# A pooling, attention and convolution backbone: the first layer's scale and shift columns as float32 matmuls with two moving columns, and the second layer's sums at other places

## The chip, the core and the metric

The program runs on one core of a Trainium2 chip. The metric is the device time of one execution in microseconds (us); lower is better. The core has five engines with a queue each: PE (matrix products; its loading of stationary operands is shown apart as PEld), DVE (VectorE), ACT (ScalarE), POOL (GpSimd) and SP, which here issues the transfers between the memory of the chip and that of the core. Each engine works through its own queue in order and waits there for what another engine has to deliver.

## What is computed

Four layers work on 1024 latent tokens with 1024 features; 256 context tokens go along through layers 0 and 1. Each layer normalises, applies a scale and a shift that depend on a condition vector, mixes the tokens, and adds the result back through a gate. The change touches only where scale, shift and gate come from, in layers 0 and 1.

```python
def _modulation(cond, w, b):
    m = jax.nn.silu(cond) @ w + b
    return jnp.split(m, 3, axis=-1)          # shift, scale, gate

shift, scale, gate = _modulation(c, ada_w[i], ada_b[i])
hx = _rmsnorm(x, norm_g[i]) * (1.0 + scale[:, None]) + shift[:, None]
cshift, cscale, cgate = _modulation(c_ctx, ada_w[i], ada_b[i])
hc = _rmsnorm(ctx, norm_g[i]) * (1.0 + cscale) + cshift
...
yx = _pool_mixer(hx, pool_w_in[j], pool_w_grp[j], pool_scale[j], pool_w_out[j])
x = x + gate[:, None] * yx
```

Layer 0 is a pooling layer: `h @ w_in` gives u and g (2048 features), u is averaged over windows of 2, 4, 8 and 16 tokens by groups of features, multiplied by `w_grp` and by silu(g), and projected by `w_out`. Layer 1 is the attention.

## The kernel before

Features lie on the 128 partitions in 8 tiles (k = 0 to 7), tokens along the rows. A float32 product is made of three products of a high and a low part (`mm3`, lines 115 to 117): a gemm of one output tile is 8 x 3 matmuls of 512 columns. The tokens are worked on in two halves of 512 (chunks 0 and 1) and the context of 256 ("c").

A column of the modulation, 128 numbers for feature tile j and one condition, is one VectorE instruction: `ada_tile` (lines 157 to 168) reads a [128, 1024] tile of the transposed weight (512 KB), multiplies it by silu of the condition, which lies on all partitions as `sil["x"]` or `sil["c"]`, and sums along the row, with the bias as start. In the trace it is `junk<-... L166`. Layer 0 has 8 scale tiles (8 to 15), 8 shift tiles (0 to 7) and 8 gate tiles (16 to 23), each for the tokens and for the context.

`consts` loads the two conditions as rows and spreads them over the partitions by four matmuls (line 569). `start` then writes out by hand what all engines but PE do, and PE's order is that of the program throughout:

- a loop over k (line 740) multiplies chunk 0 by the first five weight tiles (`FIRST`), one block of 15 matmuls per k. Ahead of block k stand the scale column of tile k + 2 (`gain`: a sum and L174), and the high and low part of the scaled x (`high` L698 on ACT, `low` L702 on DVE). The context's scale sums lie between them (`EARLY`, line 739).
- then five gemms of chunk 1 (line 822), and between them `step(k)`: the shift column of tile k for the tokens on VectorE (`ada`), and for the context on VectorE for k in 4, 6, 7 (`DV`), else as a product on GpSimd (L793) that ACT sums (L798). `rstd_chain` (lines 245 to 272) makes the inverse norms out of column sums (L240) with 12 small VectorE instructions, among which lie low parts of chunk 1; `rstd_spread` (L278) spreads them.
- then the gemms of the context for these five tiles (`shift_c` and `gained_c` make their operand; L80 of 2 columns, L805, L806).

From there `pool_in` goes on with the other eleven weight tiles; there a scheduler orders all engines but PE. Each weight tile that is fetched (`weight`, line 82) issues its transfer, is split into high and low (L79, L80), and then lets `background` do so many steps as `bg_rate` says: one step is one more modulation tile, a transfer of 512 KB and one or two sums. The steps come from `ada_all`: layer 0's gates (8 tiles, 16 sums), layer 1's scale and shift (16 tiles, 32 sums), layer 1's gate (8 tiles, 8 sums). `RATES` (line 495) holds the rate for each weight tile. Weights and modulation tiles share a ring of three buffers, `raw`. After `pool_in` come the output projection of layer 0 (`out_proj`, one step per weight tile) and layer 1.

## Time and profile before

| | |
|---|---|
| median of 3 runs | 1948.54 us (1943.30, 1948.54, 1949.06) |
| the profiled execution | 1943.86 us |
| its span from the first to the last instruction | 1942.1 us |
| PE busy in the span | 1864.4 us (96%) |
| DVE busy in the span | 1095.8 us (56%) |
| mean granted clock of TensorE | 0.985 of full speed |

The trace gives each instruction a start, a duration and an engine, and names what ended an engine's wait. TensorE's clock has two levels, 2.4 GHz (1.00 in the profile) and 1.2 GHz (0.50); the granted clock of a stretch is the mean over it. A float32 matmul that isn't split in high and low parts leaves two records per instruction, which is why four of them are counted as x8.

### The profile page before, as it was taken

To read this page: it belongs to the slowest core of one execution; us is meant where nothing else is said; L and a number is where in the kernel's file an instruction comes from. 1 tells how busy PE (TensorE), PEld (TensorE's weight loads), DVE (VectorE), ACT (ScalarE), POOL (GpSimd) and SP (SyncE) were. 2 spreads that over 40 slices of the span, in tenths; PEclk is the share of its full clock that TensorE was granted. 3 is DMA by queue.
4 is the path that set the end of the run, shared out by engine and by line. 5 is a ranking of instruction groups with operands and counts; after the bars stand their busy time and mean duration, and the time that the engine had idled before them with its cause. 6 is when DMAs were issued, how large, how long until landed. Compare 5 with 4: busy or idle time off the path is not lost.

```text
span 1942.1 us, 27112 instructions
## 1 busy us (share of the span) xinstructions
PE 1864.4 (96%) x9936; PEld 1604.0 (83%) x9936; DVE 1095.8 (56%) x2251; ACT 729.1 (38%) x1401; POOL 571.1 (29%) x552
## 2 busy tenths in 40 slices
PE   7888899999999999999998999999999999999997
PEld 4677778889998889999997877788888887888887
DVE  7989977256431066667666678544323346432627
ACT  3332215245122155666666555222212225322422
POOL 4645312652110033444433443100000024433120
PEclk9989999999999999999999999999999999999999
DMA  6233351554763466676677646443111165011234
GB/s 253 76 108 99 114 190 60 188 161 142 247 231 108 144 186 191 193 210 188 197 200 216 188 154 221 128 129 118 44 55 44 55 184 179 2 49 49 72 122 153
DMA packets 126960, 274.21 MB, mean 141 GB/s; under 512 B 12874, under 2 KB 48458, under 8 KB 126828
## 3 DMA queue, kind: packets, MB, share of 16 engines
q1 hardware_dynamic: 126828, 272.49, 44.9%
q8 instruction: 78, 1.28, 0.3%
q14 instruction: 54, 0.44, 0.1%
HBM read 218.63 MB, written 53.81 MB: 140 GB/s over the span
## 4 chain that ended last, share of the span: by engine, by line
PE 76%; DVE 12%; DMA 6%; issue 3%; POOL 2%; ACT 1%; SPq 0%; DVEq 0%; POOLq 0%; ACTq 0%
PE mm L117 22%; PE mm L115 21%; PE mm L116 21%; DVE junk L166 4%; PE T L1211 3%; PE O L1237 2%; PE O L1236 2%; DMA raw<-in_ada 2%; PE S L1154 1%; DVE S L455 1%; PE S L1155 1%; POOL S L455 1%; DMA a<-in_xT 1%; PE SC L1157 1%; PE SC L1156 1%
## 5 line engine op out<-in xcount | busy, mean ns | idle before, releaser
L115 PE MATMUL mm<-a,whi 128*128 128x512 f32 (+2 forms) x2160 | 819.9, 380 | 22.3 <-DVE U L418 10.0
L116 PE MATMUL mm<-a,whi 128*128 128x512 f32 (+2 forms) x2149 | 804.3, 374 | 10.9 <-DVE a L80 8.5
L117 PE MATMUL mm<-a,wlo 128*128 128x512 f32 (+2 forms) x2160 | 807.1, 374 | 3.5 <-POOL wlo L80 2.4
L115 PEld LDWEIGHTS mm<-a,whi 128*128 128x128 f32 x2160 | 411.5, 191 | 94.7 <-DVE U L418 11.3
L116 PEld LDWEIGHTS mm<-a,whi 128*128 128x128 f32 x2149 | 409.4, 190 | 81.0 <-DVE a L80 10.1
L117 PEld LDWEIGHTS mm<-a,wlo 128*128 128x128 f32 x2160 | 410.8, 190 | 77.9 <-POOL wlo L80 3.7
L80 POOL TENSOR_TENSOR wlo<-raw,whi 128x256 fp32r<-128x256 f32 (+2 forms) x150 | 191.0, 1288 | 382.5 <-ACT whi L79 341.9
L79 ACT ACTIVATE whi<-raw 128x1024 fp32r<-128x1024 f32 (+2 forms) x237 | 170.9, 738 | 352.1 <-PE mm L116 273.6
L166 DVE CUSTOM_DVE_ANT_0 junk<-raw,sil_x,vec 128x1024 bf16<-128x1024 f32 x86 | 117.9, 1371 | 94.4 <-DMA raw<-in_ada 94.1
L80 DVE TENSOR_TENSOR wlo<-raw,whi 128x1024 fp32r<-128x1024 f32 (+1 forms) x87 | 107.6, 1238 | 112.7 <-ACT whi L79 111.2
L1190 POOL TENSOR_SCALAR pr<-pr,rsum 128x640 f32<-128x640 f32 (+1 forms) x128 | 99.8, 779 | 238.8 <-DVE rsum L1189 188.2
L115 PE MATMUL mm<-a,a 128*128 128x512 f32 (+2 forms) x280 | 97.5, 348 | 7.4 <-ACT a L698 6.3
L1181 ACT ACTIVATE pr<-lg,nmx 128x640 f32<-128x640 f32 (+1 forms) x128 | 102.3, 799 | 2.6 <-DVE nmx L1171 1.6
L224 POOL TENSOR_TENSOR a<-a,a 128x512 f32<-128x512 f32 x42 | 59.9, 1425 | 144.2 <-ACT a L223 138.0
L116 PE MATMUL mm<-a,a 128*128 128x512 f32 (+2 forms) x275 | 95.8, 348 | 4.9 <-DVE a L702 4.9
L117 PE MATMUL mm<-a,a 128*128 128x512 f32 (+2 forms) x280 | 96.4, 344 | 0.5 <-DVE a L80 0.5
L1169 DVE TENSOR_SCALAR_CACHE_REDUCE lg<-SC 128x256 f32<-128x256 f32 x128 | 54.2, 423 | 72.9 <-PE SC L1157 72.8
L1220 DVE TENSOR_TENSOR ptlo<-T,pthi 128x512 fp32r<-128x512 f32 x128 | 88.2, 689 | 10.6 <-ACT pthi L1215 8.6
L1236 PE MATMUL O<-pthi,a 128*128 128x256 f32 x352 | 89.0, 286 | 3.2 <-ACT pthi L1215 3.2
L1237 PE MATMUL O<-ptlo,a 128*128 128x256 f32 x352 | 89.6, 289 | 1.1 <-DVE ptlo L1220 0.6
L1215 ACT ACTIVATE pthi<-T 128x512 fp32r<-128x512 f32 x128 | 76.4, 597 | 20.6 <-PE T L1211 19.5
L1211 PE MATMUL T<-ident,pr 128*128 128x128 f32 x512 | 77.6, 274 | 0.0
(182 smaller groups left out, 2495.0 us busy)
## 6 DMA issues: line engine op xcount, KB each, us to landing
raw<-in_ada SPq DMA_DIRECT2D x86, 512.0 KB
raw<-in_pool_out SPq DMA_DIRECT2D x32, 512.0 KB
raw<-in_conv_in SPq DMA_DIRECT2D x32, 512.0 KB
raw<-in_pool_in SPq DMA_DIRECT2D x27, 512.0 KB
x<-a SPq DMA_DIRECT2D x48, 256.0 KB
raw<-in_na_in SPq DMA_DIRECT2D x24, 512.0 KB
a<-dk SPq DMA_DIRECT2D x48, 256.0 KB
dv<-v SPq DMA_DIRECT2D x40, 256.0 KB
```

What stands on the lines that cost most here:

```text
L79: self.nc.scalar.activation(hi, src, AF.Copy)
L80: (lo_engine or self.nc.vector).tensor_tensor(lo, src, hi.bitcast(F32), op=ALU.subtract)
L115: t.matmul(ps, wh, hh, start=(begin and k == ks[0]), stop=False)
L116: t.matmul(ps, wh, hl, start=False, stop=False)
L117: t.matmul(ps, wl, hh, start=False, stop=(end and k == ks[-1]))
L166: nc.vector.tensor_tensor_reduce(out=junk[:], in0=raw[:], in1=self.sil[c][:], scale=1.0, scalar=self.vec[:, b:b + 1], op0=ALU.mult, op1=AL ...
L1181: nc.scalar.activation(pr[:, :L + CTX], lg[:, :L + CTX], AF.Exp, bias=nm[:], scale=-1.0, accum_out=sm[:])
L1190: nc.gpsimd.tensor_scalar(pr[:, :L], pr[:, :L], rs[:], 1.0, op0=ALU.mult, op1=ALU.mult)
L1211: nc.tensor.transpose(T[:, (s - b0) * P:(s - b0 + 1) * P], pr[:, o:o + P], self.ident[:])
L1220: nc.vector.tensor_tensor(lv, tv, hv.bitcast(F32), op=ALU.subtract)
L1236: nc.tensor.matmul(ops[:], v, hi[:, s, :], start=(n == 0), stop=False)
L1237: nc.tensor.matmul(ops[:], v, lo[:, s, :], start=False, stop=(n == len(seq) - 1))
```

## The change

1. The first layer's scale and shift columns are matmuls. `ada_product` multiplies a [128, 1024] tile of the untransposed weight (a new input, `ada0`, with the features of the condition on the partitions) as eight stationary 128 x 128 operands by `cols`, which holds silu of both conditions as two columns per feature tile. All is float32, the eight matmuls add up in one PSUM bank, and both conditions come out at once. One VectorE instruction per tile then adds the bias and, for the scale, multiplies by the norm's weight.
2. `gain(k + 1)` stands ahead of block k, where it was `gain(k + 2)`; the transfers at the start have another order, and one small transfer (`condT`) is new.
3. `RATES` and the rates at the group weights are lower, so that part of layer 1's sums falls into the output projection.

```diff
+    def ada_product(self, raw):
+        ps = self.bank()[:, 0:2]
+        for q in range(KT):
+            self.nc.tensor.matmul(ps, raw[:, q * P:(q + 1) * P], self.cols[:, 2 * q:2 * q + 2], start=q == 0, stop=q == KT - 1)
+        return ps
...
-        RATES = (0,0,0,0,3,0,5,4,3,0,6,5,5,5,8,6) if 'c' in chunks else (3, 0, 6, 6) * 4
+        RATES = (0,0,0,0,2,0,0,2,2,0,2,2,2,2,3,3) if 'c' in chunks else (3, 0, 6, 6) * 4
...
-                self.bg_rate = (3,0,0,1)[k // 2] if 'c' in chunks else 0
+                self.bg_rate = 0
...
+        self.cols = self.pc.tile([P, 2 * KT], F32, name="cols")
+        nc.sync.dma_start(self.cols[:], i["condT"])
...
+        nc.scalar.activation(self.cols[:], self.cols[:], AF.Silu)
...
         def gain(k):
-            self.ada_tile(0, ["x"], KT + k, raws[k])
-            self.gain(0, "x", k, k + 1)
+            ps = self.ada_product(raws.pop(k))
+            nc.vector.tensor_scalar(self.gains[:, :, k], ps, up[:, k:k + 1], self.vec[:, V_NG + k:V_NG + k + 1],
+                                    op0=ALU.add, op1=ALU.mult)
...
-            for q in EARLY.get(k, ()):
-                self.ada_tile(0, ["c"], KT + q, raws.pop(q))
-            if k + 2 < KT:
-                gain(k + 2)
-                high(0, x0, k + 2)
-                low(0, x0, k + 2)
+            if k + 1 < KT:
+                gain(k + 1)
+                high(0, x0, k + 1)
+                low(0, x0, k + 1)
...
-        def ada(k):
-            raw = shifts[k]
-            self.ada_tile(0, ["x", "c"] if k in DV else ["x"], k, raw)
-            if k not in DV:
-                nc.gpsimd.tensor_tensor(raw[:], raw[:], row[:], op=ALU.mult)
...
-        DV = (4,6,7,)
+        def step(k):
+            ps = self.ada_product(shifts.pop(k))
+            nc.vector.tensor_scalar(self.shifts[:, :, k], ps, self.vec[:, V_AB + k:V_AB + k + 1], None, op0=ALU.add)
...
-                for k in list(raws):
-                    self.ada_tile(0, ["c"], KT + k, raws.pop(k))
-                self.gain(0, "c")
```

In the order of the changed program, PE between the spreading of the conditions (L578 there, mm_150 and mm_151 are two of its four banks) and the second block of chunk 0 (a_207 is the scaled x of tile 0, whi and wlo the weight):

```order
L578 MATMUL mm_150<-a_137,ones 128x512
L578 MATMUL mm_151<-a_137,ones 128x512
L174 MATMUL mm_197<-cols,a_173 128x2 x8
L174 MATMUL mm_231<-cols,a_179 128x2 x8
L115 MATMUL mm_212<-a_207,whi_193 128x512
L116 MATMUL mm_212<-a_207,whi_193 128x512
L117 MATMUL mm_212<-a_207,wlo_194 128x512
...
L117 MATMUL mm_216<-a_207,wlo_194 128x512
L174 MATMUL mm_267<-cols,a_184 128x2 x8
```

Before, nothing stands between the four L569 and the first L115. Now two products (L174, x8 each) stand ahead of block 0 and one ahead of each block from block 1 to block 6; the second half of PE's part of `start` has eight more, between the gemms of chunk 1.

On VectorE, between the first spreading of inverse norms (L271) and the first chunk 0 results (U, line 418 before and 425 after), before:

```order
L271 TENSOR_SCALAR a_500<-ident,ny_498 128x128 x4
L166 ISA junk_548,M_158<-a_506,sil_x,vec 128x1024
L166 ISA M_158 128x1
L166 ISA junk_551,M_158<-a_276,a_154,vec 128x1024
L166 ISA M_158 128x1
...
L174 SCALAR_TENSOR_TENSOR A_160<-M_158,vec 128x8
L166 ISA junk_558,M_158<-a_508,sil_x,vec 128x1024
L166 ISA M_158 128x1
L418 TENSOR_TENSOR U_569<-mm_205,a_214 128x512
```

and after:

```order
L278 TENSOR_SCALAR a_550<-ident,ny_548 128x128 x4
L802 TENSOR_SCALAR M_160<-mm_598,vec 128x2
L802 TENSOR_SCALAR M_160<-mm_608,vec 128x2
L425 TENSOR_TENSOR U_624<-mm_212,a_221 128x512
```

The five long sums there are gone from VectorE, and two additions of two columns out of PSUM are left.

On SP, the first transfers of the output projection of layer 0 (in_pool_out is its weight, xo the old x; 512 KB and 256 KB), before:

```order
L86 DMA raw_2783<-in_pool_out 128x1024
L86 DMA raw_2789<-in_pool_out 128x1024
L86 DMA raw_2825<-in_pool_out 128x1024
L373 DMA xo_2795<-in_xP 128x512
L86 DMA raw_2862<-in_pool_out 128x1024
```

and after:

```order
L86 DMA raw_2807<-in_pool_out 128x1024
L162 DMA raw_2813<-in_ada 128x1024
L86 DMA raw_2819<-in_pool_out 128x1024
L162 DMA raw_2825<-in_ada 128x1024
L86 DMA raw_2861<-in_pool_out 128x1024
```

Between them and the context's gemms SP issues 32 modulation tiles before and 19 after; the other 13 (18 sums) now stand one by one between the weight tiles of the output projection, in the same ring of three buffers.

## Rows read from the trace of the kernel before

**Rows 1.** The page: busy tenths of PE and DVE in 40 slices

```profile
PE   7888899999999999999998999999999999999997
...
DVE  7989977256431066667666678544323346432627
```

**Rows 2.** Busy time by stretch: PE, PEld, DVE, ACT, POOL (x records), clock, DMA, GB/s

```profile
12.10:58.28 46.18, 36.91 (x128) 27.33 (x129) 40.18 (x45) 18.64 (x25) 24.34 (x9) 0.93 0.52 192
58.28:100.62 42.34, 34.92 (x153) 27.64 (x152) 40.96 (x76) 15.46 (x34) 25.34 (x22) 0.92 0.26 97
100.62:114.21 13.59, 6.31 (x31) 5.80 (x30) 13.48 (x24) 1.75 (x6) 3.13 (x8) 0.62 0.18 46
114.21:290.00 175.79, 158.44 (x829) 134.80 (x828) 157.23 (x254) 43.08 (x79) 72.16 (x64) 0.97 0.42 135
...
345.00:500.00 155.00, 155.00 (x1011) 142.37 (x1010) 71.71 (x146) 63.47 (x98) 70.24 (x46) 1.00 0.50 163
```

**Rows 3.** PE's waits from 12.2 to 58.2: us in total, times, longest

```profile
PE mm L115 <- ACT a L698: 11.1, 5, 2.7
```

**Rows 4.** PE's waits from 58.3 to 100.6

```profile
PE mm L116 <- DVE a L702: 4.4, 3, 2.1
PE mm L240 <- POOL a L224: 2.1, 1, 2.1
PE mm L115 <- DVE U L418: 0.9, 1, 0.9
```

**Rows 5.** PE's waits from 100.7 to 114.2

```profile
PE mm L116 <- DVE a L80: 7.3, 2, 5.2
```

**Rows 6.** PE's waits from 114.3 to 345

```profile
PE mm L115 <- DVE U L418: 9.1, 5, 4.3
...
PE mm L117 <- POOL wlo L80: 2.4, 3, 1.3
```

**Rows 7.** Timeline of PE, unsplit float32 matmuls: start us, us, engine, line, operation

```profile
55.29 0.95 PE L240 MATMUL mm<-ones,a 128*128 128x1 f32 x8
56.10 0.49 PE L115 MATMUL mm<-a,a 128*128 128x512 f32 x1
56.42 0.40 PE L116 MATMUL mm<-a,a 128*128 128x512 f32 x1
...
58.28 0.39 PE L115 MATMUL mm<-a,whi 128*128 128x512 f32 x1
...
61.01 0.40 PE L115 MATMUL mm<-a,whi 128*128 128x512 f32 x1
...
70.13 2.08 PE L278 MATMUL mm<-a,ones 128*128 128x128 f32 x8
```

**Rows 8.** Timeline of PE: the start, and stops with what followed

```profile
2.26 7.16 PE L569 MATMUL mm<-a,ones 1*128 1x512 f32 x8 [2.26 <-DMA a<-in_conds]
...
18.17 0.61 PE L116 MATMUL mm<-a,whi 128*128 128x512 f32 x1
18.60 0.43 PE L117 MATMUL mm<-a,wlo 128*128 128x512 f32 x1
...
46.05 0.79 PE L115 MATMUL mm<-a,a 128*128 128x512 f32 x1 [2.07 <-ACT a L698]
...
53.24 0.51 PE L115 MATMUL mm<-a,a 128*128 128x512 f32 x1 [1.77 <-ACT a L698]
```

**Rows 9.** Timeline from 50 to 80, DVE alone

```profile
57.75 0.15 DVE L251 TENSOR_SCALAR nv<-mm 128x4 f32<-128x4 f32 x1
57.94 2.19 DVE L253 TENSOR_SCALAR nt<-nv 128x4 int32<-128x4 int32 x1
```

**Rows 10.** The same stretch, POOL alone

```profile
57.62 2.48 POOL L734 TENSOR_TENSOR a<-a,a 128x1024 f32<-128x1024 f32 x1 [5.20 <-ACT a L730]
```

**Rows 11.** The sums (line 166) by stretch: us, DVE busy (x records), clock, DMA, GB/s

```profile
160.00:230.00 70.00, 36.56 (x48) 0.93 0.34 107
```

**Rows 12.** Groups from 340 to 460: ACT's split of the weights (busy, mean ns, idle before)

```profile
L79 ACT ACTIVATE whi<-raw 128x1024 fp32r<-128x1024 f32 x15 | 15.9, 1058 | 35.3 <-PE mm L116 35.3
```

More of the change, by code (lines that the diff above doesn't have):

```diff
@@ L560, in consts @@
         self.edge = self.pc.tile([P, 64], F32, name="edge")
+        self.cols = self.pc.tile([P, 2 * KT], F32, name="cols")
+        nc.sync.dma_start(self.cols[:], i["condT"])
         for f in range(2):
             nc.sync.dma_start(rows[f][:], i["conds"][f])
-        nc.sync.dma_start(self.x0[0], i["xT"][0, :, 0:HALF])
+        nc.scalar.activation(self.cols[:], self.cols[:], AF.Silu)
         self.ones = self.pc.tile([P, P], F32, name="ones")
@@ L576, in consts @@
         self.shifts = self.pc.tile([P, 2, 3 * KT], F32, name="M0")
+        self.gains = self.pc.tile([P, 2, KT], F32, name="A0")
         for c in range(2):
-            self.AB[0, "xc"[c]] = (self.pc.tile([P, KT], F32, name=f"A0{c}"), self.shifts[:, c, :])
+            self.AB[0, "xc"[c]] = (self.gains[:, c, :], self.shifts[:, c, :])
         for l, c in ((1, "x"), (1, "c"), (2, "x"), (3, "x")):
@@ L662, in fetch @@
             raws[k] = self.slot([P, 1024])
-            nc.sync.dma_start(raws[k][:], i["ada"][0, KT + k])
+            nc.sync.dma_start(raws[k][:], i["ada0"][KT + k])
         def fetch_w(j):
@@ L681, in start @@
             W[t] = block(t)
+        fetch(0)
+        nc.sync.dma_start(self.vec[:], i["vecs"])
         fetch_w(0)
-        nc.sync.dma_start(self.vec[:], i["vecs"])
-        fetch(0)
+        nc.sync.dma_start(x0[0], i["xT"][0, :, 0:HALF])
+        fetch(1)
         nc.sync.dma_start(x0[1], i["xT"][1, :, 0:HALF])
-        fetch(1)
         fetch_w(1)
+        fetch(2)
         self.load_pair(x0, i["xT"], 2, 0)
-        fetch(2)
+        fetch(3)
         fetch_w(2)
@@ L702, in low @@
             nc.vector.scalar_tensor_tensor(lo, x[k], A[:, k:k + 1], hi.bitcast(F32), op0=ALU.mult, op1=ALU.subtract)
+        up = self.small([P, KT], tag="up", bufs=1)
+        nc.vector.tensor_scalar(up[:], self.vec[:, V_AB + KT:V_AB + 2 * KT], 1.0, None, op0=ALU.add)
         def gain(k):
-            self.ada_tile(0, ["x"], KT + k, raws[k])
-            self.gain(0, "x", k, k + 1)
+            ps = self.ada_product(raws.pop(k))
+            nc.vector.tensor_scalar(self.gains[:, :, k], ps, up[:, k:k + 1], self.vec[:, V_NG + k:V_NG + k + 1],
+                                    op0=ALU.add, op1=ALU.mult)
         split_weight(0)
@@ L713, in start @@
             nc.scalar.activation(row[:, f * HALF:(f + 1) * HALF], self.cond[f], AF.Silu)
-        gain(1)
-        high(0, x0, 1)
-        low(0, x0, 1)
         ps = {t: self.bank() for t in tiles}
@@ L738, in start @@
         squares = {1: ((0, 0),), 2: ((0, 1),), 3: ((0, 2),), 4: ((0, 3),), 6: ((1, 0), (1, 1)), 7: ((1, 2), (1, 3))}
-        EARLY = {2: (0,), 3: (1,), 4: (2,), 5: (3,), 6: (4,)}
         for k in range(KT):
-            if k + 3 < KT:
-                fetch(k + 3)
-                if k + 3 < len(tiles):
-                    fetch_w(k + 3)
-                if k % 2:
-                    self.load_pair(x0, i["xT"], k + 3, 0)
+            if k + 4 < KT:
+                fetch(k + 4)
+                if k % 2 == 0:
+                    self.load_pair(x0, i["xT"], k + 4, 0)
+            if k + 3 < len(tiles):
+                fetch_w(k + 3)
             if k == 4:
@@ L786, in fetch_shift @@
                 shifts[k] = self.pw.tile([P, D], F32, tag="raw", name=self.nm("raw"), bufs=3)[:]
-            nc.sync.dma_start(shifts[k], i["ada"][0, k])
-        def ada(k):
-            raw = shifts[k]
-            self.ada_tile(0, ["x", "c"] if k in DV else ["x"], k, raw)
-            if k not in DV:
-                nc.gpsimd.tensor_tensor(raw[:], raw[:], row[:], op=ALU.mult)
-        def ada_sum(k):
-            raw = shifts.pop(k)
-            if k not in DV:
-                nc.scalar.activation(raw[:], raw[:], AF.Copy, accum_out=Mc[:, k:k + 1])
-                nc.gpsimd.tensor_tensor(Mc[:, k:k + 1], Mc[:, k:k + 1], self.vec[:, V_AB + k:V_AB + k + 1], op=ALU.add)
-        DV = (4,6,7,)
+            nc.sync.dma_start(shifts[k], i["ada0"][k])
+        def step(k):
+            ps = self.ada_product(shifts.pop(k))
+            nc.vector.tensor_scalar(self.shifts[:, :, k], ps, self.vec[:, V_AB + k:V_AB + k + 1], None, op0=ALU.add)
         def gained_c(k):
@@ L816, in start @@
         waiting = []
-        def step(k):
-            ada(k)
-            if k:
-                ada_sum(k - 1)
         for n, t in enumerate(tiles):
@@ L866, in start @@
                 waiting = []
-        ada_sum(7)
         shift_c(6)
@@ L1489 @@
                                 _feat(A(conv_db)), _feat(A(final_g))], axis=1),
+        "condT": np.ascontiguousarray(np.stack([_feat(A(c)), _feat(A(c_ctx))], axis=2).reshape(P, 2 * KT)),
+        "ada0": _ntiles(A(ada_w)[0, :, 0:2 * D]),
         "ada": np.ascontiguousarray(A(ada_w).transpose(0, 2, 1)).reshape(DEPTH, 24, P, D),
```

## The prediction, made before the changed kernel ran

> **What bounds the kernel now.** I read the page's busy slices first, to see where PE is not full: the first seven or so of 40 slices, some 340 us; there VectorE is at 7 to 9 tenths, and behind them PE stands at 9 throughout [rows 1]. From 345 to 500 PE is busy all the time at the full clock [rows 2]. So the change can gain only ahead of 345, and behind it can only lose. Then I cut the first part into stages with the busy times by stretch, and looked up in each what ends PE's waits and what clock was granted [rows 2 to 6]:
>
> - A, 12.1 to 58.3, chunk 0: PE waits five times, 11.1 us, for the high part on ACT [rows 3], which waits for a scale column, thus for VectorE's sums (40.2 of 46.2 us busy).
> - B, 58.3 to 100.6, chunk 1: 4.4 us for low parts, 2.1 us for column sums that GpSimd delivers late, 0.9 us for a bank [rows 4].
> - C, 100.6 to 114.2, first context gemms: 7.3 us for columns of two that stand behind sums in VectorE's queue [rows 5]; VectorE is busy 13.5 of 13.6 us and the clock is 0.62 [rows 2].
> - D, 114.2 to 290, the pooling layer: 175.8 us, of which PE is busy 158.4 and VectorE 157.2 [rows 2]; PE's longest sum of waits is for VectorE's results (9.1 us), that for GpSimd's low parts is 2.4 us [rows 6].
>
> VectorE's queue is the bound of all four, and a PE that stops often pays a second time: the mean clock is 0.92 and 0.93 in A and B and 0.97 in D [rows 2].
>
> **What the products cost.** No row shows eight stationary float32 tiles with two moving columns. The nearest shows four with one column: from 55.29 to 56.10, 0.81 us, and with 128 columns four take hardly more (2.08 us at the lower level, about twice 0.95) [rows 7]; two columns lie between. Eight are 1.62 us, and the wide matmul behind them takes 0.32 us (56.10 to 56.42) instead of 0.23 (twelve from 58.28 to 61.01), so 1.7 us each. I take 1.7; the bounds are 1.6 and 3.5 (lower clock level). Sixteen are 27 us of new PE work, and PE is now the engine that sets the pace: this is the price of the change.
>
> The Trainium skill (TensorE: Matmul & The Clock Gate, section LDWEIGHTS) gives about 107 ns for loading a 128-column stationary operand; eight loads would make 0.86 us, the sixteen products 13 us less, and the result about 1918. The rows show eight passes for four such matmuls, each near that figure, so the number of loads is what differs, and the row decides.
>
> **A.** The four spreading matmuls end at 9.4 [rows 8]; with one more small transfer ahead of them I take 9.9. Products 0 and 1 follow; both need weights that land about then (bounds: no wait, or 2 us). Before them the clock is at its lower level, as it was until 18.6, where the duration falls from 0.61 to 0.43 [rows 8]: 2 x 3.5 = 7.0, so block 0 starts at 16.9. Wide matmuls then start every 0.43 us (18.17, 18.60) [rows 8], 15 of them take 6.4, to 23.3; before, the lower level lasted 6.5 us from the first block as well. After that six products and seven blocks of 15 x 0.23 = 3.4 us [rows 7]: 10.2 + 23.8, and the column sums 0.9: A ends at 58.2. Before it ended at 58.3. So **A gains nothing**: the waits of 11 us and the low spells are filled by the products. The new chain behind a product (0.15 us on VectorE, out of PSUM, as `nv<-mm` [rows 9]; high part on ACT) has a whole block of 3.4 us to finish, so PE doesn't wait for it.
>
> **B.** Before 42.3 us. Eight products add 8 x 1.7 = 13.6. The wait of 2.1 goes (GpSimd no longer multiplies shift tiles) and the 0.9 with the sums ahead of it on VectorE. The 4.4 us stays: the low parts stand between the small instructions of the inverse-norm chain, and these are held up by GpSimd's squares, not by sums: `nt` takes 2.19 us while GpSimd works from 57.62 for 2.48, where `nv`, which reads PSUM, takes 0.15 [rows 9, 10]. With it stays the low spell behind these stops. 42.3 + 13.6 - 3.0 = 52.9, **10.6 us longer**; if waits and low spell go as well (4.4 + 2.9), 3.3 longer.
>
> **C.** VectorE has no backlog any more: from B and C some 15 long sums are gone. The 7.3 us goes, and the lower clock behind it: of the 6.3 us that PE was busy at a mean of 0.62, about 2.5 us is loss. **9.8 us shorter**; if something else on VectorE's queue (a sum whose weight tile lands late now stands between the columns of two) holds half of it, 4.9.
>
> **D.** Of 56 sums 18 move behind 290. One costs 36.56 / 24 = 1.5 us from 160 to 230 [rows 11], since each sum has two records, so 18 x 1.5 = 27 us leaves VectorE: 157.2 becomes 130 us against PE's 154 without waits and low spells (158.4 less about 4.3 us lost at the lower level, 0.03 / 0.5 x 175.8 = 10 us of which PE worked most). Now PE is the bound by a margin of 24 us. 17.3 us of waiting and 4.3 of low clock are there to be had. VectorE's 15% margin doesn't take away waits within a tile's own chain (window sums, split, products; GpSimd's 2.4 us [rows 6]). I take three quarters, **16.2 us shorter**; bounds a quarter (5.4) and all (21.6).
>
> **Behind 290.** 13 transfers and 18 sums come into the output projection, one per weight tile of 8 x 3 matmuls (5.4 us) or more. VectorE is busy 71.7 of 155 us there, and ACT's split waits 35.3 us for PE to give a buffer back, in 15 splits [rows 2, 12]: weights are ready more than two us early, each. 18 x 1.3 us of sums hides in VectorE's 83 free us: nothing. If that cover fails, see below.
>
> **Sum** against the profiled execution, 1943.86: 0 + 10.6 - 9.8 - 16.2 = -15.4, so 1928.5. That execution lies 4.7 us under the median of the three runs and 0.6 above the fastest; I add 2 for it and predict 1931. Best bounds: 3.3 - 9.8 - 21.6 = -28.1, 1915.8. Worst: 10.6 - 4.9 - 5.4 = +0.3, 1944, or 1947 at the runs' own spread.
>
> **Rivals.**
> 1. *B's waits go too and D gives all.* The chain in B starts with an emptier VectorE; against it, GpSimd's squares stand where they stood. -28, 1916 to 1920.
> 2. *D's waits only change their name.* The window sums, GpSimd and ACT take VectorE's place; for it speaks that ACT and GpSimd deliver into the same chain, against it that both are busy only 43 and 72 of 176 us [rows 2]. With a quarter of D: 10.6 - 9.8 - 5.4 = -4.6, 1939 to 1941.
> 3. *The products let the clock fall: slower.* A stop of 2.07 us (46.05) was followed by a matmul of 0.79 us, one of 1.77 us (53.24) by one of 0.51 [rows 8]: the lower level came in at the one and not at the other. A product streams 16 columns in 1.7 us; if the chip takes it for a stop, PE does A's and B's work behind block 0 (34 + 53 us) partly at 1.2 GHz. One product-and-block period in two means +44 us, 1973; the forecast's 15 us is used up as soon as 15 us of that work runs at the lower level. Against it: between products lie 3.4 to 5.4 us of dense matmuls, twice to three times the product. The Trainium skill (TensorE: Matmul & The Clock Gate, section on the second HAM failure mode) says that a PE which idles briefly between groups of matmuls often enough swings between both rates; the row at 46.05 agrees, the one at 53.24 doesn't, and no run here shows it for two moving columns.
> 4. *The output projection runs short of weights.* With modulation tiles in the ring a weight's transfer waits for a sum. If each of the 13 costs PE one sum, 13 x 1.3 = 17 us: 1945. Against it the 35.3 us that ACT waits for PE [rows 12].
> 5. *A product is cheaper than the row says* (one pass per matmul): 16 x 0.8 = 13 us more gain, 1918.
>
> **Chances.** Forecast 0.51, rival 1 0.12, rival 2 0.22, rival 3 0.07, rival 4 0.04, rival 5 0.04. 0.3%, 5.8 us, is about what a measurement of this kernel can tell from no change. Forecast, rivals 1 and 5 and half of rival 2 are faster by more: 0.78. The rest of rival 2 and most of rival 4 are within it: 0.14. Rival 3 and a bit of 4 are slower: 0.08. The range from 1916 to 1947 takes in the bounds of the terms and all but rival 3.
>
> **What would show it.** In the changed trace: eight-matmul groups of L174 with 1.6 to 1.8 us from the first to the next wide matmul (else the price was wrong). Chunk 0's blocks end near 58 and the first context gemm starts near 111, 10 us later than before, without a stop of 5 us in it. From the first context gemm to the last gemm of the pooling layer PE's waits are under 8 us instead of 25, and the granted clock is 1.00 nearly throughout. From there on PE is as full as before. The prediction is wrong if the clock is low in A or B over many products, if chunk 0 ends far from 58, or if PE's waits in D are still named after VectorE.

## The result and the profile after

The changed kernel is slower: 1968.49 us median of 4 runs (1960.89 to 1978.48) against 1946.27 us for the kernel before in the same comparison. The ratio is 1.0124, its 95% interval 1.0102 to 1.0146. Forecast was 1931 us in a range from 1916 to 1947, and faster.

The page of the changed kernel, busy tenths of PE and DVE and TensorE's clock in 40 slices (of 49 us), shows what [rows 1] showed of before. (Line numbers of the changed kernel are some 7 to 9 higher; L174 is now the product, the drains L413 and L418 are L420 and L425, L362 is L369.)

```profile
PE   9998989989999999999998998999999999999997
...
DVE  1549758566441137666666668644232336532526
PEclk9889999989999999999999999999999999999999
```

VectorE was relieved as meant: 1, 5, 4, 9 tenths in the first four slices where it had 7, 9, 8, 9. PE is fuller there (9, 9, 9, 8 instead of 7, 8, 8, 8). Yet the time is longer, so PE is full with something that isn't progress, or progress is lost elsewhere. To find where, I took the start of one and the same matmul (counted in PE's order, which is that of the program in both kernels once the products are left out) in both traces:

| the same matmul | before | after | difference | forecast of the stage |
|---|---|---|---|---|
| start of chunk 0 | 12.10 | 16.72 | +4.6 | |
| end of chunk 0 (A) | 57.35 | 57.00 | -0.4 | 0 |
| end of chunk 1 (B) | 100.17 | 122.17 | +22.0 | +10.6 |
| in the first context gemms (C) | 114.31 | 126.20 | +11.9 | -9.8 |
| the last stop of the pooling layer (D) | 289.97 | 298.54 | +8.6 | -16.2 |
| first gemm of the output projection | 334.06 | 344.62 | +10.6 | |
| first full gemm behind its column sums | 381.96 | 406.45 | +24.5 | 0 |

From there to the end the difference stays between 23 and 26 us. By stages: A -0.4, B +22.4, C -10.1, D -3.3, behind it +15.9. A and C came as forecast; B is 12 us worse, D 13 us, the output projection 16 us.

**B: the clock.** Busy times and granted clock of PE in the changed kernel by stretch (columns as in [rows 2]):

```profile
16.72:57.57 40.85, 40.85 (x224) 35.31 (x225) 12.45 (x20) 18.03 (x24) 19.86 (x9) 1.00 0.61 225
65.09:78.74 13.65, 13.28 (x50) 11.81 (x51) 4.97 (x15) 1.51 (x4) 1.77 (x6) 0.50 0.01 2
78.74:85.57 6.83, 6.83 (x43) 6.04 (x42) 2.10 (x5) 4.47 (x12) 4.06 (x10) 1.00 0.00 1
85.57:88.98 3.41, 3.41 (x11) 2.73 (x11) 2.58 (x16) 0.91 (x2) 0.00 (x0) 0.50 0.48 154
...
95.80:102.63 6.83, 6.83 (x25) 5.96 (x25) 2.49 (x14) 0.00 (x0) 0.16 (x2) 0.50 0.25 76
...
109.46:119.70 10.24, 10.24 (x38) 9.18 (x39) 4.70 (x14) 0.93 (x8) 0.00 (x0) 0.50 0.38 123
```

In chunk 0, with a product ahead of each block, the mean is 1.00 (first row). From 65 to 120 us TensorE was at 1.2 GHz for 13.7 + 3.4 + 6.8 + 10.2 = 34 us, and PE was busy nearly all that time. That is no chance of one execution: B took 64.9 to 65.6 us in the traces of five later runs whose program is the same up to there (`oldrates`, `gates_late`, `no_sums`, `half_sums`, `half_dma`). What PE did before the clock fell, in its timeline (start, us, operation; a product is 8 matmuls, x16 records):

```profile
22.12 1.84 PE L174 MATMUL mm<-cols,a 128*128 128x2 f32 x16
23.82 0.48 PE L115 MATMUL mm<-a,whi 128*128 128x512 f32 x1
...
65.06 0.79 PE L116 MATMUL mm<-a,a 128*128 128x512 f32 x1 [1.93 <-DVE a L714]
...
68.09 6.82 PE L174 MATMUL mm<-cols,a 128*128 128x2 f32 x32
...
83.10 1.84 PE L174 MATMUL mm<-cols,raw 128*128 128x2 f32 x16
84.80 1.15 PE L247 MATMUL mm<-ones,a 128*128 128x1 f32 x8
85.81 0.77 PE L115 MATMUL mm<-a,whi 128*128 128x512 f32 x1
...
92.87 1.84 PE L174 MATMUL mm<-cols,raw 128*128 128x2 f32 x16
94.57 1.03 PE L247 MATMUL mm<-ones,a 128*128 128x1 f32 x8
95.46 3.25 PE L174 MATMUL mm<-cols,raw 128*128 128x2 f32 x16
98.57 0.77 PE L115 MATMUL mm<-a,whi 128*128 128x512 f32 x1
...
106.04 1.84 PE L174 MATMUL mm<-cols,raw 128*128 128x2 f32 x16
107.74 1.14 PE L285 MATMUL mm<-a,ones 128*128 128x128 f32 x8
108.72 6.14 PE L174 MATMUL mm<-cols,raw 128*128 128x2 f32 x32
114.72 0.77 PE L115 MATMUL mm<-a,whi 128*128 128x512 f32 x1
```

A product alone takes 1.70 us (22.12 to 23.82) and is followed by full speed. The first spell, 13.7 of the 34 us, began behind a wait of 1.93 us for a low part (L714) and ahead of any product of B; the kernel before had such a spell behind such waits too, of 6.8 us (a mean clock of 0.92 over 42.3 us [rows 2]). Here the first two products stand inside it, and took 6.8 us instead of 3.4. Ahead of each of the three later spells stands a product with a column sum, a spreading matmul or another product directly behind it: 2.7 us of few columns from 83.10, then 0.50 from 85.57. Ahead of these three no row has a wait. The last two products took 6.0 us instead of 3.4.

By these rows B's 22.4 us can be added up (an estimate): eight products of 1.7 us are 13.6; 34.1 us at half speed instead of 6.8 are 13.7 more; and PE waited 2.7 us instead of 7.4 [rows 4]. That makes 22.6.

**D and the output projection: VectorE's queue.** PE's waits from the context gemms to the last stop of the pooling layer (126.2 to 298.6), the answer to [rows 6]:

```profile
PE mm L115 <- DVE U L425: 8.9, 3, 5.6
PE mm L115 <- DVE Uc L420: 3.6, 1, 3.6
PE mm L115 <- DVE a L420: 1.4, 1, 1.4
PE mm L116 <- DVE a L80: 0.4, 1, 0.4
```

14.3 us against 17.3 before. What went are the waits for ACT and GpSimd; those for drains on VectorE grew from 10.7 us to 13.9, since beside the 9.1 and 2.4 us of [rows 6] the kernel before had

```profile
PE mm L115 <- ACT a L79: 3.2, 1, 3.2
...
PE mm L115 <- DVE Uc L413: 1.6, 2, 1.3
```

And VectorE itself waits now: for modulation tiles 25.9 us in the same stretch (7.6 before, 114 to 290). Behind it PE waits once for 7.6 us, for a sum of squares (L234):

```profile
PE mm L247 <- DVE a L234: 7.6, 1, 7.6
PE mm L117 <- POOL wlo L80: 1.9, 1, 1.9
PE mm L115 <- ACT a L79: 1.8, 1, 1.8
```

That L234 stands behind this, in the timeline of VectorE in the output projection (the long sums L166, the drains L369):

```profile
391.05 2.19 DVE L166 CUSTOM_DVE_ANT_0 junk<-raw,sil_x,vec 128x1024 bf16<-128x1024 f32 x1 [3.40 <-DMA raw<-in_ada]
...
393.18 0.74 DVE L369 SCALAR_TENSOR_TENSOR a<-mm,M,xo 128x512 f32<-128x512 f32 x1
397.58 1.85 DVE L166 CUSTOM_DVE_ANT_0 junk<-raw,sil_x,vec 128x1024 bf16<-128x1024 f32 x1 [3.66 <-DMA raw<-in_ada]
...
399.36 0.74 DVE L369 SCALAR_TENSOR_TENSOR a<-mm,M,xo 128x512 f32<-128x512 f32 x1
400.86 0.69 DVE L234 TENSOR_TENSOR a<-a 128x512 f32<-128x512 f32 x1 [0.77 <-ACT a L228]
```

and this, on SP's queue (the modulation tile's transfer):

```profile
393.28 0.33 SPq L162 DMA_DIRECT2D raw<-in_ada  x1
```

The transfer goes out 0.1 us after the sum before has ended, for it takes that sum's buffer; it lands 4.3 us later; the next sum waits for it at the head of the queue, and the drain behind the sum waits with it. One turn takes 6.2 us (393.18 to 399.36). PE needs 24 x 0.23 = 5.5 us per gemm, so the drains fall behind: PE runs on without a stop from 362 to 394 us and pays at the column sums, with the stop and with a granted clock of 0.59 from 394 to 406 us.

My theory after this was: (1) products next to other few-column work let the clock fall in B; (2) the sums that were moved cost the output projection 16 us, since drains stand behind sums that wait; (3) the same eats up D's gain. The rivals stand in the expectations.

### The profile page after: what moved, and what is told of

Same layout as the page of the kernel before. It is cut to its first block, busy times and chain, and to the rows that moved or that the text cites. A ratio compares the mean times of both kernels' runs of the same rounds, so it can differ in the third digit from the quotient of the medians.

```text
span 1967.8 us, 27547 instructions
## 1 busy us (share of the span) xinstructions
PE 1903.3 (97%) x10192; PEld 1646.6 (84%) x10192; DVE 1045.5 (53%) x2205; ACT 723.5 (37%) x1392; POOL 544.5 (28%) x542
## 4 chain that ended last, share of the span: by engine, by line
PE 80%; DVE 9%; DMA 5%; issue 3%; POOL 2%; ACT 1%; SPq 0%; DVEq 0%; POOLq 0%; ACTq 0%
PE mm L115 22%; PE mm L116 22%; PE mm L117 22%; PE T L1204 3%; DVE junk L166 2%; DMA raw<-in_ada 2%; PE O L1230 2%; PE O L1229 2%; PE mm L174 2%; PE S L1147 1%; POOL wlo L80 1%; DMA a<-x 1%; PE S L1148 1%; DVE S L462 1%; DVE a L80 1%
## 5 line engine op out<-in xcount | busy, mean ns | idle before, releaser
L115 PE MATMUL mm<-a,whi 128*128 128x512 f32 (+2 forms) x2160 | 823.1, 381 | 18.5 <-DVE U L425 8.9
L115 PEld LDWEIGHTS mm<-a,whi 128*128 128x128 f32 x2160 | 413.2, 191 | 87.9 <-DVE U L425 10.0
L166 DVE CUSTOM_DVE_ANT_0 junk<-raw,sil_x,vec 128x1024 bf16<-128x1024 f32 x80 | 116.2, 1452 | 151.3 <-DMA raw<-in_ada 150.9
L115 PE MATMUL mm<-a,a 128*128 128x512 f32 (+2 forms) x280 | 96.8, 346 | 1.7 <-ACT a L79 1.7
```

The costliest lines, as they stand in the source:

```text
L115: t.matmul(ps, wh, hh, start=(begin and k == ks[0]), stop=False)
L166: nc.vector.tensor_tensor_reduce(out=junk[:], in0=raw[:], in1=self.sil[c][:], scale=1.0, scalar=self.vec[:, b:b + 1], op0=ALU.mult, op1=AL ...
```

## Experiments

Times are medians; the kernel before had 1944.5 to 1945.7 in these comparisons. "Stage" is the time between two rows of the table above, each read from one profiled execution.

**1. More columns** (`wide`): the price and the loads of a product stay, only its columns change.

```diff
-        ps = self.bank()[:, 0:2]
+        ps = self.bank()[:, 0:P]
...
-            ... self.cols[:, 2 * q:2 * q + 2], ...
+            ... self.cols[:, 2 * q:2 * q + P], ...
```

> The changed kernel with 128 moving columns per product in place of 2 (columns 0 and 1 are used, the others are neighbours and zeros that nobody reads); loads, order and rates as in the changed kernel. Theory (few moving columns let the clock fall): the spells at the lower level that began behind products at 85.6, 95.8 and 109.5 us go, a product takes 1.7 to 1.9 us, the first context gemm starts some 10 us earlier than 122 us, and the time falls from 1968 to about 1959. Rival (the loss there is the time of the products, or the stop of 1.9 us at 65 us, not the columns): the spells stay where they were, each product is 0.2 us longer, and the time is 1968 to 1972.

1951.08 us, ratio 1.0033 (1.0021 to 1.0045): 17 us better than the changed kernel, 8 more than the theory asked for. Stage B takes 52.8 us instead of 65.2. The first spell is still there, behind the same wait (1.94 us), but it ends at 70.3, in the middle of the first two products, and is about as long as in the kernel before; behind it the clock stays up:

```profile
54.91:107.17 52.26, 48.61 (x281) 42.63 (x280) 27.66 (x81) 10.97 (x30) 12.55 (x20) 0.93 0.20 69
70.33:107.17 36.84, 36.84 (x234) 33.07 (x233) 16.43 (x61) 8.37 (x26) 4.79 (x12) 1.00 0.21 65
```

A product costs the same with 128 columns, 1.70 us ahead of a wide matmul, and in the start the clock is up earlier: the first block's wide matmuls run 0.23 us apart from 16.50 on (0.43 up to 18.60 in the kernel before [rows 8], up to 20.28 in the changed kernel), so A ends 2.7 us earlier than in the changed kernel.

```profile
16.50 0.40 PE L116 MATMUL mm<-a,whi 128*128 128x512 f32 x1
16.73 0.40 PE L117 MATMUL mm<-a,wlo 128*128 128x512 f32 x1
...
19.72 1.95 PE L174 MATMUL mm<-cols,a 128*128 128x128 f32 x16
21.42 0.48 PE L115 MATMUL mm<-a,whi 128*128 128x512 f32 x1
```

**2. Two columns, other neighbours** (`apart`): each product of B stands inside a gemm.

```diff
+        MID = ({4: 0}, {3: 1, 6: 2}, {3: 3, 6: 4}, {3: 5, 6: 6}, {3: 7})
...
-            waiting.append((t, self.gemm(W[t], h, 1)))
+            mid = self.bank()
+            own = MID[n]
+            for q in range(KT):
+                if q in own:
+                    step(own[q])
+                self.mm3(mid, self.wk(W[t]), lambda kk: h[1][kk], (q,), begin=q == 0, end=q == KT - 1)
...
```

> The changed kernel with the eight shift products moved into the gemms of chunk 1, at least six wide matmuls away from the column sums, the spreading matmuls and each other, with two moving columns as before. Theory (two or more groups of few columns in a row let the clock fall, one alone between wide matmuls does not, as in chunk 0): no spell behind 79 us but the one ahead of the context gemms, the first context gemm at about 111 us in place of 122, and 1957. Rival (each product counts for the clock wherever it stands): as many spells as in the changed kernel, only at other places, and 1968.

1954.17 us, ratio 1.0043 (1.0028 to 1.0058). Stage B takes 49.1 us, and the clock is 1.00 throughout:

```profile
57.60:106.09 48.49, 46.22 (x281) 40.06 (x280) 26.87 (x81) 10.64 (x29) 12.31 (x20) 1.00 0.21 73
```

The same eight products with the same two columns, six or more wide matmuls from the next narrow group, let no clock fall. So for the three later spells (1) holds from both sides: columns and neighbours, not the products as such. For the first spell this run proves nothing, since the wait that opened it came out shorter here (0.83 and 1.05 us instead of 1.93).

**3. The rates alone** (`oldrates`: the changed kernel with this edit; `rates_only`: the kernel before with the opposite one).

```diff
-        RATES = (0,0,0,0,2,0,0,2,2,0,2,2,2,2,3,3) if 'c' in chunks else (3, 0, 6, 6) * 4
+        RATES = (0,0,0,0,3,0,5,4,3,0,6,5,5,5,8,6) if 'c' in chunks else (3, 0, 6, 6) * 4
...
-                self.bg_rate = 0
+                self.bg_rate = (3,0,0,1)[k // 2] if 'c' in chunks else 0
```

> The changed kernel with the rates of the kernel before (32 modulation tiles in the pooling layer, none in the output projection). Theory (sums that stand in VectorE's queue and wait for their transfer cost the output projection 16 us): PE runs through the output projection without a stop, as before, the pooling layer from the first context gemm on costs within 4 us of what it did, and the time is 1949 to 1955. Rival (the loss in the output projection follows from the products or from the later start, not from the sums there): the stops at 345, 356 and 402 us stay and the time is about 1968.

> The kernel before with the changed rates alone (19 modulation tiles in the pooling layer, 13 in the output projection; sums on VectorE in the first two chunks as before). Theory (the moved sums are a loss by themselves): the first 114 us are as before, the pooling layer gains 3 to 10 us, the output projection loses 16, and the time is 1952 to 1959. Rival (they are a loss only where the products empty VectorE's queue, so that it reaches a sum before its transfer has landed): 1936 to 1946.

`oldrates`: 1959.03 us, ratio 1.0067 (1.0052 to 1.0082). From the last stop of the pooling layer to the first full gemm behind the column sums it takes 93.6 us: 92.0 before, 107.9 in the changed kernel. D is 2.6 us longer than before. The time lies 4 us above what I expected, since D takes 6 us longer than in the changed kernel (178.3 and 172.3), where I had allowed less. `rates_only`: 1956.99 us, ratio 1.0065 (1.0048 to 1.0083). The first 114 us as before, D 1.1 us shorter (I had expected 3 to 10), behind it 16.1 us longer, with the changed kernel's stop (L240 and L227 here) although no product is in the program:

```profile
PE mm L240 <- DVE a L227: 7.9, 1, 7.9
```

The stretch behind D repeats well: 92.0 to 94.1 us in four traces with the old rates (before, `oldrates`, and below `gains_wide_old` and `mixed`), 107.6 to 111.2 in four with the new ones (changed, `wide`, `apart`, `rates_only`). So the rates are a loss by themselves, on either side of the products, and the rival that asked for the products falls.

**4. Sums that wait for nothing** (`landed`): the transfers stay, but each sum reads a row that already lies in the core instead of the tile transferred, so that the later modulations come out as other numbers.

```diff
-                out=junk[:], in0=raw[:], in1=self.sil[c][:], ...
+                out=junk[:], in0=self.sil["x"][:], in1=self.sil[c][:], ...
```

> The changed kernel with every sum of ada_tile (all but the first layer's scale and shift) reading a row that lies in the core, silu of the token condition, in place of the weight tile that its transfer brings; the transfers are still issued, and the modulation of the later layers is thereby another one. Theory (what PE waits for in the pooling layer and in the output projection are results that stand behind a sum in VectorE's queue, which waits for its transfer): VectorE's waits for modulation tiles vanish, PE's stops from the first context gemm to the end of the pooling layer fall from 14 us to under 6, the output projection loses under 4 us in place of 16, and the time is about 1944. Rival (the sums' own time on VectorE, or weights that come late because modulation tiles hold the ring): the stops keep at least 10 of their 14 us and the output projection 12 of its 16, and the time is 1960 to 1968.

1992.97 us, ratio 1.0247 (1.0232 to 1.0262): against the expectation. With nothing to wait for, the sums were put elsewhere by the scheduler. Busy time of line 166 by stretch (two records a sum):

```profile
0.00:149.11 149.11, 89.13 (x122) 0.82 0.35 127
149.11:313.23 164.12, 27.47 (x38) 0.97 0.29 89
313.23:405.20 91.97, 0.00 (x0) 1.00 0.59 191
```

61 sums stand in the first two chunks, where VectorE then stops PE (the first 149 us are 35 us longer than in the kernel before). As a test of D it fails. Of the stretch behind D it says something: 12 modulation transfers go out there, as many as in the changed kernel and in the same ring, no sum is there, and it takes 91.9 us, as before. The transfers alone cost nothing; the price is the sums, or what they hold back. Which of the two this run doesn't tell: as no sum reads a tile here, no transfer of a weight has to wait for a sum either.

**5. Where in the output projection** (`gates_late`): the eight tiles of layer 1's gate, one sum each, move behind the output projection.

```diff
-        self.bg = [self.ada_all(0, (2,), (2,)), self.ada_all(1, (0, 1), (0, 1)), self.ada_all(1, (2,))]
+        self.bg = [self.ada_all(0, (2,), (2,)), self.ada_all(1, (0, 1), (0, 1))]
...
     def na_first(self, h):
+        self.bg = [self.ada_all(1, (2,))]
```

> The changed kernel with layer 1's gate (8 tiles, one sum each) taken out of the output projection and put behind it, at the beginning of layer 1's first part; 5 tiles with 10 sums stay in the output projection. Theory (the stop of 7.6 us at 402 us and the lower clock behind it are the drains that stand behind those eight waiting sums): this stop goes, some 10 us, the stops at 345 and 356 us stay, layer 1 loses less than 3 us, and the time is 1957 to 1961. Rival (they only move their waits into layer 1): 1966 to 1970.

1963.52 us, ratio 1.0100 (1.0081 to 1.0118). The stop of 7.6 us is gone (the stretch takes 100.6 instead of 107.9), but layer 1 loses 7 us where I had allowed 3: PE waits 3.3 and 1.4 us there for the spreading of the inverse norms, which VectorE makes. So in the trace the gain is lost again and the rival is right: the sums carry their price along. (Its profiled execution took 1970.4 us, the longest of its four. The median lies 5 us under the changed kernel's, but the intervals of the two ratios overlap, so whether anything was gained is not shown.)

**6. No sums, half sums, half transfers** (`no_sums`, `half_sums`, `half_dma`): what in D is the price? The first leaves out layer 0's gate and layer 1's modulation, transfers and sums, and has constants in their place. The second sums 512 of the 1024 columns of a whole tile. The third transfers half of each tile and reads it twice. What the three compute is something else; only their times count.

```diff
+        if l < 2:
+            return
```

```diff
-                out=junk[:], in0=raw[:], in1=self.sil[c][:], ...
+                out=junk[:, 0:512], in0=raw[:, 0:512], in1=self.sil[c][:, 0:512], ...
```

```diff
-            nc.sync.dma_start(raw[:], self.i["ada"][l, j])
+            nc.sync.dma_start(raw[:, 0:512], self.i["ada"][l, j][:, 0:512])
...
+                ... in0=raw[:, 0:512].unsqueeze(1).broadcast_to((P, 2, 512)), ...
```

> The changed kernel without layer 0's gate and layer 1's modulation: their 32 transfers and 56 + 18 - 18 = 56 long sums (38 in the pooling layer, 18 behind) are left out and the columns are constants. Theory (the sums in VectorE's queue, by their waits and their time, are what stops PE from the context gemms to the end of the output projection): the first 126 us stay as in the changed kernel, the stops up to the end of the pooling layer fall from 14 us to under 4 and the low clock goes, the output projection has none, and the time is 1968 - 12 - 16 = 1940 (1936 to 1945). Rival (window sums, splits and products of a tile are the chain there, sums or not): at least 8 us of stops stay in the pooling layer, and 1948 or more.

> The changed kernel with every sum of ada_tile over 512 of the 1024 columns; the transfers are whole, so that a sum waits as long but takes half the time. Theory (the wait for the transfer is the price): the output projection still loses at least 12 of its 16 us, the pooling layer's stops stay over 9 of 14 us, and the time is 1960 to 1968. Rival (the time of the sums is the price): the output projection loses 8 us or less, the pooling layer's stops halve, and the time is 1948 to 1956.

> The changed kernel with half of each modulation tile transferred (256 KB) and read twice by the sum, so that a sum of ada_tile takes as long as in the changed kernel and its transfer half as much. With whole transfers and half sums the pooling layer took 162 us from its first to its last stop's place (172 in the changed kernel, 157 without sums) and the output projection lost 12 us. Theory (wait and sum stand one behind the other in VectorE's queue, and a stop is what of both exceeds PE's lead): the pooling layer takes 162 to 168 us, the output projection loses 4 to 8 us, and the time is 1948 to 1956. Rival for the pooling layer (the sums' time alone is the price there): it stays at 170 to 174 us, and the time is 1956 or more. Rival for the output projection (the order of the queue, not the length of a transfer): it keeps 12 us or more.

Medians 1935.30 (0.9959, 0.9943 to 0.9975), 1953.79 (1.0045, 1.0031 to 1.0060) and 1971.13 us (1.0129, 1.0112 to 1.0146). D in thirds, by the starts of the same four matmuls (114.31, 168.94, 230.10 and 289.97 in the trace of before), and the stretch behind D, in us:

| | D 1 | D 2 | D 3 | D | behind |
|---|---|---|---|---|---|
| before (15, 19, 22 sums in the thirds) | 54.6 | 61.2 | 59.9 | 175.7 | 92.0 |
| changed (8, 8, 18) | 52.3 | 53.8 | 66.2 | 172.3 | 107.9 |
| no sums | 52.4 | 51.0 | 53.8 | 157.1 | 91.9 |
| half sums | 52.5 | 51.5 | 58.0 | 162.0 | 103.8 |
| half transfers | 52.6 | 55.6 | 64.4 | 172.6 | 111.0 |

Without sums one wait is left in D, for GpSimd's low part:

```profile
PE mm L117 <- POOL wlo L80: 4.0, 2, 3.8
```

So the sums are what stops PE, and the rival of experiment `no_sums` (the tiles' own chain) falls. But the waits for transfers are not the price in D: with half sums VectorE waits longer for them than in the changed kernel (33.5 us instead of 25.9 in D, 68.6 instead of 57.9 up to 400), and D still gains 10 us more. With half transfers it gains nothing. There theory (3) falls in the form in which I stated it: D and the time of `half_sums` came as its rival had them, while the output projection kept 11.8 of its 15.9 us, near what the theory had. My expectation of `half_dma` falls too: both rivals there were right. In D's last third the sums of the changed kernel do wait for their transfers,

```profile
266.18 1.28 DVE L166 CUSTOM_DVE_ANT_0 junk<-raw,sil_x,vec 128x1024 bf16<-128x1024 f32 x1 [3.67 <-DMA raw<-in_ada]
...
272.85 1.28 DVE L166 CUSTOM_DVE_ANT_0 junk<-raw,sil_x,vec 128x1024 bf16<-128x1024 f32 x1 [3.71 <-DMA raw<-in_ada]
```

yet that third is 8.2 us shorter with half sums and only 1.8 with half transfers. The timeline of `half_dma` shows why shorter transfers don't help the output projection:

```profile
389.92 3.43 DVE L166 CUSTOM_DVE_ANT_0 junk<-raw,sil_x,vec 128x1024 bf16<-128x1024 f32 x1 [2.17 <-DMA raw<-in_ada]
...
393.29 0.74 DVE L369 SCALAR_TENSOR_TENSOR a<-mm,M,xo 128x512 f32<-128x512 f32 x1
```

```profile
388.62 1.30 POOL L231 TENSOR_TENSOR a<-a,a 128x512 f32<-128x512 f32 x1 [2.63 <-ACT a L230]
389.88 2.40 POOL L80 TENSOR_TENSOR wlo<-raw,whi 128x1024 fp32r<-128x1024 f32 x1
```

In the changed kernel the same split, and a sum with none beside it, read

```profile
389.77 2.39 POOL L80 TENSOR_TENSOR wlo<-raw,whi 128x1024 fp32r<-128x1024 f32 x1
```

```profile
403.68 1.28 DVE L166 CUSTOM_DVE_ANT_0 junk<-raw,sil_x,vec 128x1024 bf16<-128x1024 f32 x1 [2.13 <-DMA raw<-in_ada]
```

With half the transfer the tile lands earlier (the wait is 2.17 us instead of 3.40), but the sum then runs while GpSimd splits a weight, and takes 3.43 us, where the changed kernel's, which began later in the same split, took 2.19, and one with no split beside it 1.28. Either ends 1.0 us behind the split's end: at 393.29, where the changed kernel's ended at 393.18. A turn goes from the drain over ACT's and GpSimd's squares and split to the sum's end, and remains 6.2 us. The Trainium skill (GPSIMD Engine Reference, section 1, Specifications) lists GpSimd's access to the core's memory as shared with VectorE, with contention for instructions with two such inputs; a sum has two, and the row at 389.92 agrees.

**7. Versions** (`best24`, `gains_wide_old`, `mixed`). The first puts the shift products apart, uses 128 columns, 24 modulation tiles in the pooling layer and layer 1's gate behind it. The second keeps only the scale columns as products (128 columns) and takes shift sums and rates from the kernel before. The third adds to the second three shift tiles as products apart. The rates of the first, the step of the second and the edit of the third:

```diff
-        RATES = (0,0,0,0,2,0,0,2,2,0,2,2,2,2,3,3) if 'c' in chunks else (3, 0, 6, 6) * 4
+        RATES = (0,0,0,0,2,0,0,3,2,0,3,3,3,2,3,3) if 'c' in chunks else (3, 0, 6, 6) * 4
```

```diff
         def step(k):
-            ps = self.ada_product(shifts.pop(k))
+            ada(k)
+            if k:
+                ada_sum(k - 1)
```

```diff
-        DV = (4,6,7,)
+        DV = ()
...
+        PROD = {2: 4, 3: 6, 4: 7}
+                if q == 4 and n in PROD:
+                    product(PROD[n])
```

> The version with all that the runs so far showed: shift products apart in the gemms of chunk 1, 128 moving columns in all products, 24 modulation tiles in the pooling layer, none in the output projection, and layer 1's gate behind it. By theory the first full gemm behind the context starts 5 to 8 us earlier than before, the pooling layer gains or loses up to 3 us, the output projection loses nothing, and the time is 1936 to 1942. Rival (the wait for transfers in the pooling layer grows with the room that VectorE has): 1942 to 1950.

> The scale columns alone as products, with 128 moving columns each; the shift columns are sums on VectorE and GpSimd and the rates are those of the kernel before. By theory chunk 0 ends 3 us earlier than before (as with 128 columns in all products), chunk 1 costs what it did before less the waits for sums of the scale, and the first context gemms wait less: the first full gemm behind them starts 3 to 12 us earlier than before, the pooling layer and the output projection cost what they did before, and the time is 1934 to 1942. Rival (the columns for the context's operand wait for the shift sums as before): 1942 to 1946.

> As gains_wide_old (scale columns as products with 128 moving columns, rates of the kernel before), but the shift tiles 4, 6 and 7, whose two sums each stand on VectorE ahead of the context's operand, are products too, one in the middle of each of the last three gemms of chunk 1. By theory the three products cost 3 x 1.9 = 5.7 us in chunk 1 and take away the two waits of 7.4 us for columns and the lower clock around the context gemms (10 us at half speed, of which about 4 us loss), the first full gemm behind the context starts 3 to 6 us earlier than there, and the time is 1931 to 1935. Rival (the columns then wait for GpSimd's and ACT's sums of the others): 1937 to 1942.

`best24`: 1952.06 us, ratio 1.0033 (1.0021 to 1.0046), above both ranges that I had given. C ends 7.1 us earlier than before, as expected, but D gives back 5.1 (one stop of 8.8 us at 260 us), the output projection 1.8 and layer 1 6. `gains_wide_old`: **1937.15 us, ratio 0.9958 (0.9944 to 0.9971), faster than both kernels**, if by 0.4% only, and as expected. C ends 8.9 us earlier than before, D costs what it did (176.1 us), and behind it 2.1 us go. `mixed`: 1938.13 us, ratio 0.9969 (0.9957 to 0.9982). The three products take the waits in C away, as expected (C ends 12.5 us earlier than before), but D takes 181.3 us and gives 5.6 back, so that the time is 3 us above the range expected. Why D gives it back there, and not in `gains_wide_old`, stays open.

## Why the prediction was wrong, point by point

- **A: right.** Block 0 was forecast at 16.9 us and began at 16.72; the end was forecast at 58.2, and with the difference of -0.4 measured it is 57.9. That it fits so closely is in part luck: block 0 took 5.4 us instead of 6.4 (the lower level ended at 20.7), and the other blocks with their products 0.9 us longer than forecast. A product was forecast at 1.7 us and took 1.70. `wide` adds that it isn't the columns that cost: 128 take no longer. (Of the 11.1 us of waits that the prediction gives to A, 2.7 had ended by 12.10, where A begins, and the clocks of A and B are exchanged in its text; neither changes its sum.) The figure of the Trainium skill that I had weighed (TensorE: Matmul & The Clock Gate, section LDWEIGHTS; 0.86 us per product by it) would have been half of that; the trace doesn't agree.
- **C: right.** -9.8 forecast, -10.1 measured. The waits of [rows 5] for columns in VectorE's queue are gone.
- **B: the step that failed** is that products in chunk 1 cost 1.7 us each and leave the clock alone. I had that mechanism as rival 3 with a chance of 0.07, and argued it away with "between products lie 3.4 to 5.4 us of dense matmuls". That is true of A, where no spell came. In B the order of PE's queue, which stands in the program, has products directly ahead of column sums, spreading matmuls and each other; I priced them one by one and never listed their neighbours. TensorE stood at the lower level for 34 us of B instead of 6.8, which cost 13.7 us. Where the clock stayed up behind the products (`wide`), B took 52.8 us, which is the 52.9 that I had forecast. That rival 3's own time, 1973 us, lies near the measured one is luck: it had half of A and B at the lower level, 44 us, and nothing lost in D or behind it. The rule of the Trainium skill that I named beside that rival (TensorE: Matmul & The Clock Gate, section on the second HAM failure mode) speaks of short idle times between groups; the rows here go further, since PE didn't idle ahead of 85.57 at all.
- **D: the step that failed** is "now PE is the bound by a margin of 24 us", worked out from busy sums over 176 us. VectorE did come down as forecast, from 157 busy us to 128, and PE still waited 13.9 us for its drains. PE's stops there aren't made by VectorE's total but by what stands ahead of one drain: the 22 sums that left D in the changed kernel (18 in the forecast) gave 3 us, the other 34 would give 15. The rates did win 9.7 us in D's first two thirds, 2 us short of what half sums gave there, and lost 6.4 in the last, although that third has 18 sums instead of 22. There VectorE has caught up with the transfers and waits for them (the rows at 266.18 and 272.85), but halving the sums shortened that third by more than halving the transfers did (8.2 and 1.8 us), so the sums' own time counts there more than the wait. Why the kernel before, with more sums, loses less there (its rates put up to six modulation tiles in a row, without a weight between them in the ring) stays open. Rival 2 ("the waits only change their name") came nearest, with -4.6 in its sum, but by the reverse of its mechanism: it had GpSimd and ACT take VectorE's place, and it was their waits that went and VectorE's drains that stayed.
- **Behind 290: the step that failed** is that VectorE's 83 free us and ACT's 35.3 us of waiting for PE [rows 2, 12] cover 18 sums. They cover their time, not their place: a sum at the head of the queue holds the drain behind it until its transfer has landed, and that transfer goes out only when a buffer of the ring comes free. A shorter transfer doesn't help (`half_dma`), as the sum then stands still beside GpSimd's split, and a sum of half the length only by 4 us (`half_sums`). `oldrates` and `rates_only` put 14 to 16 us on the rates that brought the sums there, and `landed` shows the transfers harmless without them. Rival 4 had the sum nearly (17 us) by another path, weights that come late; in the changed kernel PE waits there for a weight once, 1.9 us, and for the drains 7.6.

The sum of the stages, -0.4 + 22.4 - 10.1 - 3.3 + 15.9 = +24.5, is nearly all of the difference of the spans (1967.8 - 1942.1 = 25.7). The range failed with it: B lies 12 us outside the bounds that the prediction had set for it, D 2 us, and the stretch behind 290 had none, since its cost was put at nothing.

## What to carry to other kernels

Where narrow matmuls are put between wide ones, list what stands next to each in PE's queue: one narrow group of 1.7 us among wide ones cost only its time, two in a row cost as much again in clock, and filling the moving operand to 128 columns kept the clock up at no price here. Long background work that waits for a transfer should not stand ahead of a drain in an in-order queue: it holds the drain by its wait and by its own time, and the runs here put more on its time in D and on its place in the output projection. Free time of the engine says nothing about it, and neither does the sum of its work. Before moving background work, look at whose buffer its transfer takes, and at which moment that comes free.

## What the runs showed of the hardware that I had not expected

- The clock fell to 1.2 GHz without any stop of PE: behind 83.10 us PE issued a product and a column sum without a gap, and the granted clock was 0.50 from 85.57 to 88.98. With 128 columns in the products it stayed at 1.00 in the same order, from 70.33 to 107.17.
- A float32 product of eight stationary tiles takes 1.70 us with 2 and with 128 moving columns (22.12 to 23.82 in the changed kernel, 19.72 to 21.42 in `wide`).
- A sum of VectorE over 1024 columns took 1.28 us alone and 3.43 us beside one 2.40 us split on GpSimd; it ended 1.0 us behind the split's end, however early it had begun.
